# Hymba block with hierarchical mixture of experts: the final norm of all rows moved into the last two experts' products, and those experts' rows gathered, summed, normed and stored over the others

## The chip, the cores and the metric

The kernel runs on one core of a Trainium2 chip. The metric is the device time of one execution in microseconds (us). Engines: PE (TensorE, matmuls; PEld are its weight loads), DVE (VectorE), ACT (ScalarE), POOL (GpSimd), SP (SyncE, which here only issues DMAs). A queue issues its DMAs in the order written; POOL issues the indirect ones (gathers and scatters by a list of row numbers).

## The reference, cut to what matters

One layer over 1024 rows of 1024 numbers: a mixer, a cross attention, then a mixture of experts, and a last RMS norm. Each row goes to one of 4 groups and to 2 of the 4 experts in it, so two experts of different groups never share a row.

```
def hierarchical_moe(h, ...):
    ...
    for e in range(N_EXPERTS):                       # 16
        hid = jax.nn.silu(t @ w_gate[e]) * (t @ w_up[e])
        out = out + combine[:, e:e + 1] * (hid @ w_down[e])
...
    x = x + hierarchical_moe(rms_norm(x, ffn_norm[l]), ...)
return rms_norm(x, final_norm)                       # y * rsqrt(mean(y * y) + eps) * gain
```

## The kernel before, in words

Up to about 780 us the kernel does the mixer, the attention and the routing. It leaves the normed rows in a DRAM buffer `h3d` and the rows so far in a DRAM buffer `acd`, both with 128 spare rows behind the 1024. The experts follow in the order of `ORDER` (L39): 0, 4, 8, 12, 1, ... 3, 7, 11, 15, so neighbours are of different groups. `p` is expert 11 and `LAST` is 15.

An expert takes up to 128 rows as its first slot and up to 64 more as its second; all work of the second slot stands in a branch, `second(e)` (L1207), that is taken only where the expert has more than 128 rows. Empty places of a slot hold row numbers from 1024 up: a gather reads spare rows there, a scatter writes nothing (`bounds_check`). A loop for experts with still more rows (`others`, L1221) isn't entered.

Per expert (loop at L1323): `gate_up` (L1126) for 8 pieces of the gate and up weights, `hidden` (silu and product, L1130), the same for the second slot (`gate_up2`, L1171, `hidden2`), the turning of the next expert's rows, then `down` (L1143) of the expert before, whose 128 weighted rows `add_rows` (L1198) adds into `acd` by an indirect DMA that accumulates; `over` (L1135) turns and splits the hidden rows for `down`; `down2` and `rows2` (L1191, L1194) do the second slot, followed by a second `add_rows`. Each float32 factor is split into a high part (ACT, L163) and a low part (DVE, L169), and a product is three matmuls (`six`, L1119).

The weights are a list of jobs, each a piece of 512 KB. `Weights` (L1260) holds 9 raw buffers (`RAW`) and the other free slots as pairs for split pieces. `load` (L1285) issues on SP while there is a job and a raw buffer; `split(n)` (L1292) splits up to n loaded pieces while a pair is free, gives the raw buffer back and calls `load`. The list (L659) is written out by hand: per expert its 8 gate and up pieces and the 4 down pieces of the expert before; for the last expert the down pieces come first.

`tc.manual_schedule()` (L1312, L1477) keeps each engine's instructions in the order written. The waits between them, DMAs to DRAM included, are put in for every pair of accesses that overlap.

After the loop: down products of 11, its two `add_rows`, then gate and up of 15, the load of all of `acd` into eight tiles `acc` (L1401 to L1403), `over` and down of 15. The rows of 15 aren't added in DRAM: matrices `oh` with a one where row number and slot agree (L1411) place them by matmuls (`placed`, L1433). `MODES` (L57) gives each of the eight tiles a way to the norm: in A DVE adds the placed rows to `acc` (`added`, L1447), ACT squares and sums (L1459), POOL takes the root (L1461), DVE scales and applies the gain `fn` (L1467); in B the add is a matmul with the identity (L1445) and DVE scales from PSUM (L1470). SP stores the tile to `out` (L1475).

Of the kernel before, what the change touches and what calls it, by code (L numbers as in the profile page):

```python
# [8 lines left out]
F32 = mybir.dt.float32  # L9
F32R = mybir.dt.float32r  # L10
# [43 lines left out]
C_N = C_WR + ND * 24  # L54


MODES = "ABABABAB"  # L57
START = 12
FILL = 2
LAG = 2  # L60


class Slots:
# [22 lines left out]
def block_kernel(ctx: ExitStack, tc: tile.TileContext, A):  # L86
# [572 lines left out]
    for s, e in enumerate(ORDER):  # L659
        gu = [("gu", e, k) for k in range(ND)]  # L660
        dn = [("dn", ORDER[s - 1], k) for k in range(4)] if s else []
        for name, i, k in dn + gu if s == NE - 1 else gu + dn:
            W.add((name, i, k), A["w_" + name][i, k])
    for k in range(4):
        W.add(("dn", ORDER[-1], k), A["w_dn"][ORDER[-1], k])
# [541 lines left out]
    def second(e):  # L1207

        return tc.If((flags & (1 << e)) > 0, preferred_fallthrough_block=True)

    hrow = [half.get() for _ in range(2)]
    routed = half.get(BF16, (P, P))
    act.copy(routed, idf)
# [98 lines left out]
    with tc.manual_schedule():  # L1312
        flags = nc.values_load(two[0:1, 0:1], engines=(PE, ACT, DVE), min_val=0, max_val=(1 << NE) - 1)
        X = Weights(W.jobs, W.flying, W.ready, RAW)
        X.load()
        x0 = x0_bufs[0]
        run(turned(x0, xg[0]))
        with second(ORDER[0]):
            turned2()
        for i in range(2):  # L1320
            fetch(ORDER[1], i)
        pool.memset(og[1][LO], 0.0)
        for s, e in enumerate(ORDER[:-1]):  # L1323
            p = ORDER[s - 1] if s else None
            nx = ORDER[s + 1]
            for k in range(ND):
                gate_up(x0, X.get(("gu", e, k)), k)
                X.split(1)
            hidden()
            ws = [X.get(("gu", e, k)) for k in range(ND)]  # L1330
            with second(e):
                for k in range(ND):
                    gate_up2(ws[k], k)
                hidden2(slot(e, 1)[1])
            for k in range(ND):
                X.drop(("gu", e, k))
            x0 = x0_bufs[(s + 1) % 2]
            ops = turned(x0, xg[0])
            if s + 2 < NE:
                fetch(ORDER[s + 2], 0)  # L1340
            run(ops)
            X.split(2)
            if p is not None:
                wd = [X.get(("dn", p, k)) for k in range(4)]
                for k in range(4):
                    down(wd[k], k)
                X.split(1)
                weighted(slot(p, 0)[1])
                add_rows(slot(p, 0)[0], og[0])
            over()  # L1350
            X.split(2)
            if p is not None:
                with second(p):
                    for k in range(4):
                        down2(wd[k], k)
                    rows2(og[1])
                add_rows(slot(p, 1)[0][LO], og[1][LO])
                for k in range(4):
                    X.drop(("dn", p, k))
            with second(e):  # L1360
                over2()
            with second(nx):  # L1362
                turned2()
            if s + 2 < NE:
                fetch(ORDER[s + 2], 1)


        p, LAST = ORDER[-2:]
        wd = [X.get(("dn", p, k)) for k in range(4)]
        for k in range(4):  # L1370
            down(wd[k], k)
        X.split(1)
        weighted(slot(p, 0)[1])
        add_rows(slot(p, 0)[0], og[0])
        with second(p):
            for k in range(4):
                down2(wd[k], k)
            rows2(og[1])
        add_rows(slot(p, 1)[0][LO], og[1][LO])
        for k in range(4):  # L1380
            X.drop(("dn", p, k))
        slots.put(*xg, *x0_bufs[NE % 2])
        fn, row = slots.get(), slots.get()
        oh = slots.get(F32R), slots.get(F32R)
        pool.iota(row, pattern=[[1, T]], base=0, channel_multiplier=0, allow_small_or_imprecise_dtypes=True)
        pool.dma_start(fn, A["final_norm"])
        for k in range(ND):
            gate_up(x0, X.get(("gu", LAST, k)), k)
            X.split(2)
        hidden()  # L1390
        ws = [X.get(("gu", LAST, k)) for k in range(ND)]
        with second(LAST):
            for k in range(ND):
                gate_up2(ws[k], k)
            hidden2(slot(LAST, 1)[1])
        for k in range(ND):
            X.drop(("gu", LAST, k))
        assert not X.jobs
        X.split(4)
        wd = [X.get(("dn", LAST, k)) for k in range(4)]  # L1400
        acc = [X.place(X.raw, F32) for _ in range(NT)]  # L1401
        for t in range(NT):
            sp.dma_start(acc[t], acd[cut(t), :])  # L1403
        over()
        with second(LAST):
            over2()
        slots.put(*x0, xp)
        slots.free.extend(X.raw)
        ogs = [[slots.get(F32R) for _ in range(2)] for _ in range(2)]
        for i in range(2):  # L1410
            dve.tensor_scalar(oh[i], row, idf[:, LAST * 8 + i:LAST * 8 + i + 1], None, op0=ALU.is_equal)  # L1411
        with second(LAST):
            for k in range(4):
                down2(wd[k], k)
            rows2(og[1])
            split(ogs[1][0][LO], ogs[1][1][LO], og[1][LO])
        for k in range(4):
            down(wd[k], k)
        for n in range(2):
            split(ogs[0][0][:, HS[n]], ogs[0][1][:, HS[n]], dn_banks[n], slot(LAST, 0)[1])  # L1420
        for k in range(4):
            X.drop(("dn", LAST, k))
        slots.free.extend(X.pair)
        slots.put(*og, hid, hp)
        banks.put(*gu_banks, *dn_banks, *turn_banks)

    ssf = const.tile([P, 2 * NT], F32, name="ssf")
    rf = const.tile([P, NT], F32, name="rf")  # L1430
    pss, jk = {}, {}

    def placed(t):  # L1433
        jk[t] = slots.get()
        pss[t] = [banks.get() for _ in range(2)]
        for n, ps in enumerate(pss[t]):
            pe.matmul(ps, oh[0][:, cut(t)], ogs[0][0][:, HS[n]], start=True, stop=False)
        with second(LAST):
            for n, ps in enumerate(pss[t]):
                for o in ogs[1]:  # L1440
                    pe.matmul(ps, oh[1][LO, cut(t)], o[LO, HS[n]], start=False, stop=False)
        for n, ps in enumerate(pss[t]):
            pe.matmul(ps, oh[0][:, cut(t)], ogs[0][1][:, HS[n]], start=False, stop=MODES[t] != "B")  # L1443
            if MODES[t] == "B":
                pe.matmul(ps, ident, acc[t][:, HS[n]], start=False, stop=True)  # L1445

    def added(t):  # L1447
        if MODES[t] != "B":
            for n, ps in enumerate(pss[t]):
                dve.tensor_tensor(acc[t][:, HS[n]], ps, acc[t][:, HS[n]], op=ALU.add)  # L1450

    def summed(t):
        r, s2 = rf[:, t:t + 1], [ssf[:, 2 * t + n:2 * t + n + 1] for n in range(2)]
        if MODES[t] == "B":
            for n, ps in enumerate(pss[t]):
                act.activation(jk[t][:, HS[n]], ps, AF.Square, scale=1.0 / 32.0, accum_out=s2[n])  # L1456
            pool.tensor_scalar(r, s2[0], s2[1], EPS, op0=ALU.add, op1=ALU.add)  # L1457
        else:
            act.activation(jk[t], acc[t], AF.Square, scale=1.0 / 32.0, accum_out=s2[0])  # L1459
            pool.tensor_scalar(r, s2[0], EPS, None, op0=ALU.add)  # L1460
        pool.tensor_tensor(r, r, mhalf[:, 0:1], op=ALU.pow)  # L1461
        slots.put(jk[t])

    def scaled(t):
        r = rf[:, t:t + 1]
        if MODES[t] == "A":
            dve.scalar_tensor_tensor(acc[t], acc[t], r, fn, op0=ALU.mult, op1=ALU.mult)  # L1467
        elif MODES[t] == "B":
            for n, ps in enumerate(pss[t]):
                dve.scalar_tensor_tensor(acc[t][:, HS[n]], ps, r, fn[:, HS[n]], op0=ALU.mult, op1=ALU.mult)  # L1470
        else:
            act.activation(acc[t], acc[t], AF.Copy, scale=r)
            pool.tensor_tensor(acc[t], acc[t], fn, op=ALU.mult)
        banks.put(*pss[t])
        sp.dma_start(A["out"][cut(t), :], acc[t])  # L1475

    with tc.manual_schedule():  # L1477
        for t in range(NT + LAG):
            if t < NT:
                placed(t)  # L1480
                added(t)
                summed(t)
            if t >= LAG:
                scaled(t - LAG)


def layout(inputs):
# [63 lines left out]
```

## Time and profile before

| | |
|---|---|
| median of 3 runs | 1225.35 us (1223.7 to 1225.55) |
| the profiled execution | 1224.64 us, of which the span is 1222.9 us |
| PE busy in the span | 1178.0 us, 96% |
| DVE busy | 712.3 us, 58% |
| ACT busy | 567.5 us, 46% |
| POOL busy | 188.6 us, 15% |
| read from HBM, written | 173.49 MB, 29.62 MB |

Times in rows are us from the start of the span. A busy share is an average over stages with different limits; the rows of a stage tell what bounds it. DMA-issuing instructions aren't counted as busy. A wait is put down to the releaser that came last by the profile; where the engine named had long been done, it was another, often a DMA.

### The profile page before, as it was taken

How to read it: one execution, taken by the hardware profiler on the slowest of the kernel's cores; microseconds unless marked ns; L12 is line 12 of the kernel's file. 1: busy time of each engine (PE TensorE's matmuls, PEld its weight loads, DVE VectorE, ACT ScalarE, POOL GpSimd, SP SyncE). 2: the span in 40 equal slices, each digit the busy share in tenths (PEclk: the TensorE clock that was granted, in tenths of full speed). 3: DMA queues.
4: the chain of work that ended last, by engine and by line, in shares of the span. 5: the costliest groups of instructions: out<-in, count | busy, mean ns of one | idle time of the engine just before them, and what ended most of it. 6: DMA issues, size and time to landing. Idle time of an engine off the chain costs nothing. (4 is left out here: it accounts for less than half of the span.)

```text
span 1222.9 us, 20592 instructions
## 1 busy us (share of the span) xinstructions
PE 1178.0 (96%) x7918; PEld 966.8 (79%) x7918; DVE 712.3 (58%) x1162; ACT 567.5 (46%) x965; POOL 188.6 (15%) x229
## 2 busy tenths in 40 slices
PE   9999999999999999999999999789999999999985
PEld 7787878787889988898888888568787777787762
DVE  6625454547457512364454776756867768668645
ACT  6613232323335402463244443545866767658633
POOL 1100101010100100100001333212223222123122
PEclk9999999999999999999999999889999999999988
DMA  9601110111426811120032321667979779798764
GB/s 343 240 18 48 41 54 35 36 53 54 157 85 242 281 63 35 35 104 1 1 121 83 125 104 70 218 232 242 317 245 377 254 263 349 255 338 290 247 176 194
DMA packets 58316, 196.48 MB, mean 161 GB/s; under 512 B 8925, under 2 KB 9565, under 8 KB 58208
## 3 DMA queue, kind: packets, MB, share of 16 engines
q1 hardware_dynamic: 45216, 157.69, 35.2%
q0 software_dynamic: 12704, 37.26, 10.4%
q8 instruction: 68, 1.11, 0.4%
q14 instruction: 40, 0.33, 0.1%
q10 hardware_dynamic: 288, 0.09, 0.0%
HBM read 173.49 MB, written 29.62 MB: 166 GB/s over the span
## 5 line engine op out<-in xcount | busy, mean ns | idle before, releaser
L257 PE MATMUL b<-s,s 128*128 128x512 f32 (+1 forms) x1056 | 402.7, 382 | 0.9 <-ACT s L165 0.8
L259 PE MATMUL b<-s,s 128*128 128x512 f32 (+1 forms) x1056 | 392.6, 372 | 0.0
L258 PE MATMUL b<-s,s 128*128 128x512 f32 (+1 forms) x1056 | 392.1, 371 | 0.1
L169 DVE TENSOR_TENSOR s<-s,s 128x1024 fp32r<-128x1024 f32 (+2 forms) x272 | 315.1, 1203 | 57.1 <-ACT s L163 35.4
L163 ACT CAST s<-s 128x1024 fp32r<-128x1024 f32 (+2 forms) x272 | 268.2, 1042 | 133.5 <-PE b L259 47.7
L1124 PE MATMUL b<-s,s 128*128 128x512 f32 x1152 | 275.3, 397 | 4.5 <-PEq L1362 1.7
L1124 PEld LDWEIGHTS b<-s,s 128*128 128x128 f32 x1152 | 217.0, 191 | 51.9 <-ACT s L163 2.7
L259 PEld LDWEIGHTS b<-s,s 128*128 128x128 f32 x1056 | 199.0, 188 | 35.4 <-issue 0.2
L257 PEld LDWEIGHTS b<-s,s 128*128 128x128 f32 x1056 | 199.0, 189 | 33.5 <-ACT s L165 1.5
L258 PEld LDWEIGHTS b<-s,s 128*128 128x128 f32 x1056 | 199.5, 189 | 31.3 <-DVE s L171 1.0
L169 DVE TENSOR_TENSOR s<-b,s 128x512 fp32r<-128x512 f32 (+1 forms) x112 | 70.9, 647 | 45.5 <-ACT s L163 42.5
L1200 POOL DMA_INDIRECT acd<-s,idi x30 | 59.2, 1972 | 204.9 <-ACT s L1148 66.4
L1163 PE MATMUL b<-s,s 128*128 128x512 f32 x384 | 90.5, 391 | 0.0
L1163 PEld LDWEIGHTS b<-s,s 128*128 128x128 f32 x384 | 71.6, 188 | 14.7
L163 ACT CAST s<-b 128x512 fp32r<-128x512 f32 (+1 forms) x112 | 60.7, 558 | 42.6 <-PE b L264 16.6
L1106 POOL DMA_INDIRECT s<-h3d,idi x32 | 37.1, 1160 | 106.4 <-PE b L1114 87.3
L1175 ACT COPY h<-b 64x512 f32<-64x512 f32 x32 | 18.6, 582 | 67.7 <-PE b L1163 57.0
L1176 DVE TENSOR_TENSOR h<-b,h 64x512 f32<-64x512 f32 x16 | 10.9, 682 | 63.1 <-ACT h L1175 63.1
L784 DVE TENSOR_TENSOR s<-b,s 128x512 f32<-128x512 f32 x16 | 11.0, 691 | 58.7 <-PE b L259 58.6
L264 PE MATMUL b<-ident,s 128*128 128x128 f32 x288 | 40.9, 273 | 1.0 <-DVE s L615 0.9
L547 DVE TENSOR_TENSOR s<-s,s 128x512 f32<-128x512 f32 x28 | 19.3, 691 | 37.6 <-PE b L538 22.1
L264 PEld LDWEIGHTS b<-ident,s 128*128 128x128 f32 x288 | 34.5, 140 | 8.0 <-DVE s L615 1.3
(232 smaller groups left out, 920.2 us busy)
## 6 DMA issues: line engine op xcount, KB each, us to landing
s<-in_w_gu_dram SPq DMA_DIRECT2D x128, 512.0 KB, 6.8
s<-in_w_dn_dram SPq DMA_DIRECT2D x64, 512.0 KB, 7.5
s<-in_w_in_dram SPq DMA_DIRECT2D x26, 512.0 KB, 3.5
s<-in_w_kv_dram SPq DMA_DIRECT2D x16, 512.0 KB, 5.5
h3d<-s POOLq DMA_DIRECT2D x9, 512.0 KB, 3.1
acd<-s POOLq DMA_DIRECT2D x9, 512.0 KB, 3.2
s<-in_xT_dram SPq DMA_DIRECT2D x16, 256.0 KB, 5.5
s<-in_x_dram SPq DMA_DIRECT2D x8, 512.0 KB, 9.0
```

What stands on the lines that cost most here:

```text
L163: act.copy(hi, src)
L169: (eng or dve).tensor_tensor(lo, src, hi.bitcast(F32), op=ALU.subtract)
L257: pe.matmul(ps, lh, rh, start=first, stop=False)
L258: pe.matmul(ps, lh, rl, start=False, stop=False)
L259: pe.matmul(ps, ll, rh, start=False, stop=last)
L264: pe.transpose(pt[:, cut(c)], src[:, cut(half * 4 + c)], ident)
L547: dve.tensor_tensor(k4[:, :, 0, :], k4[:, :, 0, :], tv[:, :, 1:2].to_broadcast([P, nb, w]), op=ALU.mult)
L1106: pool.indirect_dma_start(out=to, out_offset=None, in_=h3d, in_offset=rows, bounds_check=T - 1, oob_is_err=False)
L1124: pe.matmul(ps[n], l, r[:, HS[n]], start=a, stop=b)
L1163: pe.matmul(ps[n], l, r[:, HS[n]], start=first and i == 0, stop=last and i == 1)
L1175: act.copy(up2[UP], ps[UP])
L1200: pool.indirect_dma_start(out=acd, in_=src, in_offset=None, compute_op=ALU.add, out_offset=rows, bounds_check=T - 1, oob_is_err=False)
```

## The change

The final norm's modes are now A (as before, but with nothing to add) and C: ACT scales by the root, POOL multiplies by the gain. The weights of 11's down product move behind 15's gate and up pieces. The down product of 11 moves behind gate and up of 15. Four tiles of `acc` take the slots of the gathered rows and of the turned rows that are no longer needed, four more take raw weight buffers as these come free; `residual` loads them from `acd`, which by then lacks the rows of 11 and 15. Those experts' rows are gathered out of `acd` into `ax` (four gathers), the weighted products are added there (`first_sum`, `second_sum`), and they are normed by themselves (`again` names their columns, `first_out`, `second_out`); `store` writes them with indirect DMAs over the rows that the eight tiles' stores have written. The one-hot matrices, `placed` and `added` go, and with them 11's `add_rows`. The functions of the tail that are removed are those printed above (`placed` to the end, L1429 to L1484); they stand as "..." in the diff.

```
@@ -54,10 +54,9 @@
 C_N = C_WR + ND * 24
 
 
-MODES = "ABABABAB"
+MODES = "ACACACAC"
 START = 12
 FILL = 2
-LAG = 2
 
 
 class Slots:
@@ -659,7 +658,7 @@
     for s, e in enumerate(ORDER):
         gu = [("gu", e, k) for k in range(ND)]
         dn = [("dn", ORDER[s - 1], k) for k in range(4)] if s else []
-        for name, i, k in dn + gu if s == NE - 1 else gu + dn:
+        for name, i, k in gu + dn:
             W.add((name, i, k), A["w_" + name][i, k])
     for k in range(4):
         W.add(("dn", ORDER[-1], k), A["w_dn"][ORDER[-1], k])
@@ -1208,6 +1207,9 @@
 
         return tc.If((flags & (1 << e)) > 0, preferred_fallthrough_block=True)
 
+    ssf = const.tile([P, NT + 8], F32, name="ssf")
+    rf = const.tile([P, NT + 4], F32, name="rf")
+    pool.memset(ssf, 1.0)
     hrow = [half.get() for _ in range(2)]
     routed = half.get(BF16, (P, P))
     act.copy(routed, idf)
@@ -1365,28 +1367,96 @@
                 fetch(ORDER[s + 2], 1)
 
 
+
         p, LAST = ORDER[-2:]
-        wd = [X.get(("dn", p, k)) for k in range(4)]
-        for k in range(4):
-            down(wd[k], k)
-        X.split(1)
-        weighted(slot(p, 0)[1])
-        add_rows(slot(p, 0)[0], og[0])
-        with second(p):
-            for k in range(4):
-                down2(wd[k], k)
-            rows2(og[1])
-        add_rows(slot(p, 1)[0][LO], og[1][LO])
-        for k in range(4):
-            X.drop(("dn", p, k))
+        assert p // 4 != LAST // 4
         slots.put(*xg, *x0_bufs[NE % 2])
-        fn, row = slots.get(), slots.get()
-        oh = slots.get(F32R), slots.get(F32R)
-        pool.iota(row, pattern=[[1, T]], base=0, channel_multiplier=0, allow_small_or_imprecise_dtypes=True)
-        pool.dma_start(fn, A["final_norm"])
+        acc = [slots.get() for _ in range(4)]
+
+        def residual(ts):
+            for t in ts:
+                sp.dma_start(acc[t], acd[cut(t), :])
+
+        def root(r, *ss):
+            if len(ss) == 2:
+                pool.tensor_scalar(r, ss[0], ss[1], EPS, op0=ALU.add, op1=ALU.add)
+            else:
+                pool.tensor_scalar(r, ss[0], EPS, None, op0=ALU.add)
+            pool.tensor_tensor(r, r, mhalf[0:r.shape[0], 0:1], op=ALU.pow)
+
+        def squares(a, ss):
+            act.activation(jk[0:a.shape[0], 0:a.shape[1]], a, AF.Square, scale=1.0 / 32.0, accum_out=ss)
+
+        def summed(t):
+            squares(acc[t], ssf[:, t:t + 1])
+            root(rf[:, t:t + 1], ssf[:, t:t + 1])
+
+        def scaled(t):
+            r = rf[:, t:t + 1]
+            if MODES[t] == "A":
+                dve.scalar_tensor_tensor(acc[t], acc[t], r, fn, op0=ALU.mult, op1=ALU.mult)
+            else:
+                act.activation(acc[t], acc[t], AF.Copy, scale=r)
+                pool.tensor_tensor(acc[t], acc[t], fn, op=ALU.mult)
+            sp.dma_start(A["out"][cut(t), :], acc[t])
+
+        def final(ts):
+            for i, t in enumerate(ts):
+                summed(t)
+                if i:
+                    scaled(ts[i - 1])
+            scaled(ts[-1])
+
+        def again(j, i):
+
+            c = NT + 2 * j + i
+            return rf[:, c:c + 1], [ssf[:, NT + 4 * j + 2 * i + n:NT + 4 * j + 2 * i + n + 1] for n in range(2)]
+
+        def first_sum(j, e):
+            a, (r, ss) = ax[j][0], again(j, 0)
+            for n in range(2):
+                dve.scalar_tensor_tensor(a[:, HS[n]], dn_banks[n], slot(e, 0)[1], a[:, HS[n]],
+                                         op0=ALU.mult, op1=ALU.add)
+                squares(a[:, HS[n]], ss[n])
+            root(r, *ss)
+
+        def second_sum(j, e, wd):
+            a, (r, ss) = ax[j][1][LO], again(j, 1)
+            with second(e):
+                for k in range(4):
+                    down2(wd[k], k)
+                rows2(og[1])
+                dve.tensor_tensor(a, a, og[1][LO], op=ALU.add)
+                squares(a, ss[0][LO])
+            root(r[LO], ss[0][LO])
+
+        def store(ix, src):
+            rows = bass.IndirectOffsetOnAxis(ap=ix, axis=0)
+            pool.indirect_dma_start(out=A["out"], in_=src, in_offset=None, out_offset=rows,
+                                    bounds_check=T - 1, oob_is_err=False)
+
+        def first_out(j, e):
+            a, r = ax[j][0], again(j, 0)[0]
+            dve.scalar_tensor_tensor(a, a, r, fn, op0=ALU.mult, op1=ALU.mult)
+            store(slot(e, 0)[0], a)
+
+        def second_out(j, e):
+            a, r = ax[j][1][LO], again(j, 1)[0]
+            with second(e):
+                dve.scalar_tensor_tensor(a, a, r[LO], fn[LO], op0=ALU.mult, op1=ALU.mult)
+            store(slot(e, 1)[0][LO], a)
+
         for k in range(ND):
             gate_up(x0, X.get(("gu", LAST, k)), k)
-            X.split(2)
+            X.split(1)
+            if not X.jobs and len(acc) == 4:
+                residual(range(4))
+            if len(X.raw) >= 5 and len(acc) == 4:
+                acc += [X.place(X.raw, F32) for _ in range(4)]
+                residual(range(4, NT))
+                fn = X.place(X.raw, F32)
+                pool.dma_start(fn, A["final_norm"])
+        assert not X.jobs and len(acc) == NT
         hidden()
         ws = [X.get(("gu", LAST, k)) for k in range(ND)]
         with second(LAST):
@@ -1395,93 +1465,33 @@
             hidden2(slot(LAST, 1)[1])
         for k in range(ND):
             X.drop(("gu", LAST, k))
-        assert not X.jobs
         X.split(4)
-        wd = [X.get(("dn", LAST, k)) for k in range(4)]
-        acc = [X.place(X.raw, F32) for _ in range(NT)]
-        for t in range(NT):
-            sp.dma_start(acc[t], acd[cut(t), :])
+        wd, wl = ([X.get(("dn", e, k)) for k in range(4)] for e in (p, LAST))
+        slots.free.extend((*X.pair, *X.raw))
+        jk = slots.get()
+        ax = [[slots.get() for _ in range(2)] for _ in range(2)]
+        for j, e in enumerate((p, LAST)):
+            for i in range(2):
+                ix, to = (slot(e, 1)[0][LO], ax[j][1][LO]) if i else (slot(e, 0)[0], ax[j][0])
+                pool.indirect_dma_start(out=to, out_offset=None, in_=acd,
+                                        in_offset=bass.IndirectOffsetOnAxis(ap=ix, axis=0))
+        final(range(0, 3))
+        for k in range(4):
+            down(wd[k], k)
         over()
+        first_sum(0, p)
+        second_sum(0, p, wd)
         with second(LAST):
             over2()
-        slots.put(*x0, xp)
-        slots.free.extend(X.raw)
-        ogs = [[slots.get(F32R) for _ in range(2)] for _ in range(2)]
-        for i in range(2):
-            dve.tensor_scalar(oh[i], row, idf[:, LAST * 8 + i:LAST * 8 + i + 1], None, op0=ALU.is_equal)
-        with second(LAST):
-            for k in range(4):
-                down2(wd[k], k)
-            rows2(og[1])
-            split(ogs[1][0][LO], ogs[1][1][LO], og[1][LO])
+        final(range(3, NT))
+        first_out(0, p)
+        second_out(0, p)
+        second_sum(1, LAST, wl)
+        second_out(1, LAST)
         for k in range(4):
-            down(wd[k], k)
-        for n in range(2):
-            split(ogs[0][0][:, HS[n]], ogs[0][1][:, HS[n]], dn_banks[n], slot(LAST, 0)[1])
-        for k in range(4):
-            X.drop(("dn", LAST, k))
-        slots.free.extend(X.pair)
-        slots.put(*og, hid, hp)
-        banks.put(*gu_banks, *dn_banks, *turn_banks)
...
+            down(wl[k], k)
+        first_sum(1, LAST)
+        first_out(1, LAST)
```

## Rows read from the trace of the kernel before

**Rows 1.** The page's first line: the span.
```profile
span 1222.9 us, 20592 instructions
```
**Rows 2.** Windows: stretch, length, busy PE, PEld, DVE, ACT, POOL, clock, DMA, GB/s.
```profile
1150.00:1180.00 30.00, 27.34 (x120) 21.16 (x118) 19.09 (x22) 20.53 (x27) 7.14 (x5) 1.00 0.48 123
...
1193.00:1213.00 20.00, 16.72 (x48) 8.41 (x48) 15.28 (x20) 10.18 (x25) 6.88 (x15) 1.00 0.53 214
```
**Rows 3.** Timeline of PE: start, us, line, operation, count, idle before.
```profile
1157.14 5.95 PE L1124 MATMUL b<-s,s 128*128 128x512 f32 x24 [0.42 <-ACT s L163]
...
1162.93 3.79 PE L1163 MATMUL b<-s,s 128*128 128x512 f32 x16
...
1166.56 5.60 PE L1124 MATMUL b<-s,s 128*128 128x512 f32 x24
...
1184.71 7.73 PE L1124 MATMUL b<-s,s 128*128 128x512 f32 x24 [0.72 <-ACTq L1405]
```
**Rows 4.** The stores to out: issue in ns, first and last start; landing.
```profile
L1475 SPq DMA_DIRECT2D out_dram<-s x8: 332/332/451, 1201.6 to 1215.1; - x8
...
DMA to landing us min/median/max: 2.6/2.7/3.3
```
**Rows 5.** Timeline of SP's DMA issues, from 1156.
```profile
1156.49 4.33 SPq L1289 DMA_DIRECT2D s<-in_w_dn_dram  x4
...
1183.53 5.05 SPq L1403 DMA_DIRECT2D s<-acd  x8
```
**Rows 6.** Waits of SP's queue: us in total, times, longest.
```profile
SPq L1403 <- DMA acd<-s,idi: 22.3, 1, 22.3
```
**Rows 7.** Timeline of POOL: expert 7's second row addition, expert 11's first.
```profile
1167.85 1.43 POOL L1200 DMA_INDIRECT acd<-s,idi  x1 [8.81 <-DMA acd<-s,idi]
...
1171.11 1.56 POOL L1200 DMA_INDIRECT acd<-s,idi  x1 [1.82 <-DMA acd<-s,idi]
```
**Rows 8.** Windows of 2 us while the eight loads of acc run.
```profile
1186.00:1188.00 2.00, 2.00 (x6) 1.52 (x6) 0.95 (x2) 0.00 (x0) 0.00 (x0) 0.50 1.10 309
...
1190.00:1192.00 2.00, 2.00 (x10) 1.66 (x9) 0.00 (x0) 0.00 (x0) 0.00 (x0) 1.00 1.02 416
```
**Rows 9.** DMA queues from 1100 to 1150: packets, MB, share of 16 engines.
```profile
q1 hardware_dynamic: 3456, 12.58, 65.4%
...
q0 software_dynamic: 896, 2.32, 19.4%
```
**Rows 10.** Groups by line and shape: busy us, mean ns of one, idle before.
```profile
L169 DVE TENSOR_TENSOR s<-s,s 128x1024 fp32r<-128x1024 f32 x14 | 16.2, 1215 | 0.7 <-ACT s L163 0.4 <-DVEq L1362 0.3
...
L1459 ACT ACTIVATE s<-s 128x1024 f32<-128x1024 f32 x4 | 4.2, 1057 | 7.7 <-DVE s L1450 6.0 <-issue 1.8
...
L1459 ACT ACTIVATION_READ_ACCUMULATOR s<-s 128x1 f32 x4 | 0.7, 186 | 0.0
...
L1461 POOL TENSOR_TENSOR rf<-rf,mhalf 128x1 f32<-128x1 f32 x8 | 4.5, 565 | 0.7
...
L1467 DVE SCALAR_TENSOR_TENSOR s<-s,rf,s 128x1024 f32<-128x1024 f32 x4 | 5.1, 1276 | 0.0
...
L171 DVE SCALAR_TENSOR_TENSOR s<-b,wts,s 128x512 fp32r<-128x512 f32 x2 | 1.4, 746 | 6.0 <-ACT s L165 6.0
...
L961 POOL TENSOR_TENSOR s<-s,s 128x512 f32<-128x512 f32 x8 | 10.4, 1302 | 8.3 <-ACT s L960 8.3
...
L1175 ACT COPY h<-b 64x512 f32<-64x512 f32 x3 | 1.7, 582 | 2.3 <-DVE s L1176 2.3
```
**Rows 11.** Issue to landing, us: gathers, additions at 1167.85 and 1171.11, acc loads.
```profile
s<-h3d,idi POOLq DMA_INDIRECT x2, 4.6
...
acd<-s,idi POOLq DMA_INDIRECT x1, 2.5
...
acd<-s,idi POOLq DMA_INDIRECT x1, 6.2
...
DMA to landing us min/median/max: 5.6/8.2/10.1
```

More of the change, by code (lines that the diff above doesn't have):

```diff
@@ L1417, in block_kernel @@
-        for k in range(4):
-            down(wd[k], k)
-        for n in range(2):
-            split(ogs[0][0][:, HS[n]], ogs[0][1][:, HS[n]], dn_banks[n], slot(LAST, 0)[1])
-        for k in range(4):
-            X.drop(("dn", LAST, k))
-        slots.free.extend(X.pair)
-        slots.put(*og, hid, hp)
-        banks.put(*gu_banks, *dn_banks, *turn_banks)
[L1429 to L1484, printed above, removed]
+        final(range(3, NT))
[3 more added lines that the diff above has]
+        second_out(1, LAST)
+        for k in range(4):
+            down(wl[k], k)
+        first_sum(1, LAST)
+        first_out(1, LAST)
 def layout(inputs):
```

## The prediction, made before the change was run

> **What bounds the kernel now.** I read the page first: 1222.9 us of span [rows 1]. The profiled execution took 1224.64 us, so 1.74 us lie around the span, and it stands 0.71 us below the 1225.35 us median. All sums below are made against 1224.64. About 0.2%, 2.4 us, is what a measurement can tell from no change.
>
> Next I read the windows by stage. Until 1180 PE is busy 27.3 of 30 us; from 1193 to 1213 it shares the work with DVE at 15.3 of 20 [rows 2]. The change touches only what follows 1157, so the PE rows from there come third: the products of expert 11 (the kernel's `p`, 24 big matmuls and 16 for its second rows), the first half of expert 15's gate and up, and, after a break, expert 15's down product at half clock, 7.73 us [rows 3]. Expert 15 (`LAST`) has no second rows: no L1163 follows. After 1193 comes the tail that the change replaces: placing by one-hot products, norm, stores; the last store is issued at 1215.1 and the span ends 7.8 us later [rows 4].
>
> Then the queues. SP issues its last weight load by 1160.8 and nothing more until 1183.5 [rows 5]; it is held 22.3 us there, by the landing of the last row addition into `acd` [rows 6]. POOL shows why: each addition starts only when the one before it has landed [rows 7].
>
> **What goes.** The eight placings (48 matmuls), `added`, and the two one-hot builds: from 1193 to 1215, 22 us on the path. Expert 11's two row additions, from 1171.1 on, go too, so the rows of `acd` are final when expert 7's second addition lands, at 1171.1 [rows 7]. The products close up: gate and up of 15 from 1157.1 take 11.2 us (two halves of 5.6), down of 11 takes 5.9, its second rows 3.8 [rows 3], so PE is free near 1178. If nothing else held it, down of 15 would end near 1184, 8 us earlier than now. The new order of the weight list costs nothing: as many loads and splits come at each place, and seven of 15's eight pieces are already split when the loop ends. Without that cover each piece would cost a split, 1.2 us on DVE. The memset of 16 columns lies beside the routing; the iota and the one-hot builds that go were on no path.
>
> **What comes first: the loads of `acc`.** Follow `residual(range(4))` through the gate and up loop of 15. Its condition is that no weight is left to issue and that `acc` still has four tiles. The weight list is empty before the loop begins [rows 5]. Raw buffers were all in flight; each turn frees one, so five are free only in the fifth turn, when `acc` grows. The condition is therefore true in turns one to five, and the same four loads are issued **five times**: 20 loads of 0.524 MB, then the other four, where eight were issued before. Each repeat overwrites the same tile, so it waits for the load before it to land, and the first norm waits for the fifth. Nothing else is queued behind SP but the stores.
>
> Time of acc[0]: start at 1171.2, when the addition has landed. Sixteen loads and its own make 17. The rate where SP's loads are alone on the DMA engines is 416 GB/s [rows 8], so 1.26 us each, 21.4 us; four in flight cover the reissue. Fixed part: a store of the same size lands in 2.7 us [rows 4], so 1.4 besides its transfer. POOL's four gathers move 384 rows, 1.57 MB, on the same engines; in an earlier stretch POOL's queue took 19.4% for 2.32 MB where SP's took 65.4% for 12.58 [rows 9], over 50 us that is 4.2 against 2.6 us a MB, so 6.6 us (4.1 at SP's price). `final_norm` lands before. acc[0] is ready at 1171.2 + 21.4 + 1.4 + 6.6 = 1200.6; the lower bound is 1197, from the gathers at SP's price and one of them before the loads. Here a rule speaks for a later time. The Trainium skill, DMA: Bandwidth & Descriptors, section Where 436 GB/s comes from, says that transfers between HBM and SBUF are bound at about 358 GB/s. By it acc[0] would be ready 3.6 us later; the row disagrees, and the row is used.
>
> **What waits for acc[0].** The engines run in written order. ACT's first norm square stands ahead of `over`, both sums and the later norms, so ACT, then DVE and POOL, hold still from about 1172 to 1200.6. PE does down of 11 and its second rows, then waits for ACT's split of 15's hidden rows, some 25 us; its clock was at half after the break before down of 15 too [rows 8], where the 24 matmuls took 7.73 us for 5.95 [rows 3]. A longer break may make it 10 us; it lies beside work that ends later.
>
> **The tail from acc[0], T0.** Durations [rows 10]: square 1.06 + 0.19; root 0.57, with the small add before it and handoffs 0.9; scaling on DVE 1.28; ACT's copy is taken as the square's 1.06. POOL's multiply by `fn` has no row at 1024 columns; twice the 512-column row is 2.6 (0.4 either way, an estimate: a start shared by the halves, or DVE beside it). Three squares and a copy: 5.0. `over` and the halves of `first_sum` of 11 (0.75 on DVE, 0.78 on ACT): 9.3. The branch, two second-row sums (0.58 on ACT, at most 0.75 on DVE), an add of 1.2, a square of 1.25, the untaken branch: T0 + 15.6. Then five tiles, held by POOL: two squares 2.5, copy 1.2, multiply 2.7, root 0.9, copy 1.2, multiply 2.6, root 0.9, copy 1.2, multiply 2.6, in all 15.8, and store and landing 2.8: T0 + 34.2. The Trainium skill, GPSIMD Engine Reference, section Elementwise — side-by-side cycle accounting, states 4497 ns for 2048 columns; half of it, 2.25 us as an estimate, would end the tail 1.0 us sooner. No row here shows that size.
>
> Then four scatters into `out`. They overlap all stores to `out`, as the additions overlap in `acd`, so the first waits for the last store and each for the one before. A plain scatter has no row. Nearest: a plain gather lands 4.6 us after issue, an addition that writes no row 2.5 (3.3 between starts), an adding scatter of 128 rows 6.2 [rows 7, 11]. I take 4.6 with 0.3 of handoff, 4.4 for 64 rows; bounds 3.3 and 6.2. Eleven's two: 9.3. Fifteen's second scatter writes no row, 1.4 of POOL; the last root is queued behind it, 1.2, then DVE's scaling 1.3 and the last scatter 4.6. The last row lands at T0 + 51.9. From the last landing to the span's end it was 5.1 us (7.8 less 2.7) [rows 4].
>
> **Sum:** 1200.6 + 51.9 + 5.1 = 1257.6 of span, + 1.74 = **1259 us**, 2.8% slower. The work removed from the path (22 us) is outweighed: the norms start 22 us after the products of 11, and the tail behind their start is 57 us.
>
> **Rivals.** (a) Each round waits out a whole landing. The eight loads of before landed in a median 8.2 us, the first in 5.6 [rows 11]; four rounds of 8.2 and one of 5.6 give acc[0] at 1209.6: 1268. For it: reissue needs a semaphore and SP's turn. Against: four in flight hold 5 us of transfer, more than 2.7.
> (b) Scatters into `out` are not held by the stores or by each other, since no row shows an order on `out`: the last lands at T0 + 44.2, 1252. Against: [rows 7].
> (c) The other side: the loads are issued once, that is, five raw buffers are free in the first turn. Its place is the first pass of the condition, its price 25.5 us: acc[0] at 1175, and 1234 with my tail. The length of the tail decides: up to 45 us after acc[0] (mine is 51.9) it ends within 0.2% of before, and with the short scatters of (b), 44.2, at **1226, not slower**. For it: eight loads would do all the work. Against: the count of free buffers, and SP's rows [rows 5].
> (d) Multiply and scatters at their upper bounds: T0 + 56.8, 1264.
>
> **Numbers.** Forecast with its bounds 0.60; (a) 0.12; (b) 0.12; (c) 0.07, of which 0.03 within 0.2% and 0.02 faster; (d) 0.07; 0.02 faster for what I have not seen. So faster 0.04, same 0.03, slower 0.93. The forecast's bounds are -3.5 for the loads and -5.2 to +4.9 for the tail; (a) reaches 1268; (b), with the gathers wholly ahead of the loads (-6.6) and the multiply low (-1.2), 1244. The range is 1243 to 1269.
>
> **What would show it.** SP issues 24 loads from `acd`, with about 25 us of waits on their own landings; ACT, DVE and POOL stand still from about 1172 to 1200; PE has one gap of over 20 us before down of 15, at half clock after it; POOL's three multiplies lead the five norms; four scatters close the chain, POOL waiting for DMA. Eight loads, or a first square before 1180, would make the step on the loads wrong; scatters that start before the last store lands, the step on their order.

## The result, and the profile after

Median 1266.71 us (1266.33 to 1267.62, 4 runs) against 1224.53 us (1221.64 to 1225.55, 4 runs) for the kernel before on the same chip: ratio 1.035, 95% interval 1.033 to 1.0369. The forecast was 1259 us, with a range of 1243 to 1269. The profiled execution is the one of 1267.62 us; 1.8 us of it lie around the span. Its page begins:

```profile
span 1265.8 us, 20509 instructions
```

against [rows 1]. The windows by stage, in the columns of [rows 2]:

```profile
1180.00:1190.00 10.00, 0.28 (x2) 0.00 (x0) 0.00 (x0) 0.00 (x0) 0.00 (x0) 0.67 1.02 317
1190.00:1200.00 10.00, 0.00 (x0) 0.00 (x0) 0.00 (x0) 0.00 (x0) 0.00 (x0) 0.50 1.01 392
1200.00:1206.00 6.00, 0.00 (x0) 0.00 (x0) 0.00 (x0) 0.00 (x0) 0.00 (x0) 0.50 1.02 410
1206.00:1243.00 37.00, 7.38 (x24) 5.47 (x24) 15.52 (x14) 19.13 (x33) 22.70 (x24) 0.59 0.50 200
1243.00:1266.00 23.00, 0.00 (x0) 0.00 (x0) 1.28 (x1) 0.00 (x0) 5.71 (x8) 0.50 0.15 53
```

For 26 us no engine computes and the DMA engines are full: the kernel waits for data. Then follow 37 us in which no engine is full, POOL the busiest, and 23 us of almost nothing. The timeline of SP, where [rows 5] had eight loads in 5.05 us:

```profile
1174.72 32.57 SPq L1378 DMA_DIRECT2D s<-acd  x24
1209.78 30.01 SPq L1401 DMA_DIRECT2D out_dram<-s  x8
```

and the waits of SP's queue, in the columns of [rows 6]:

```profile
SPq L1378 <- DMA s<-acd: 23.2, 16, 3.2
...
SPq L1378 <- DMA acd<-s,idi: 11.3, 1, 11.3
```

There are 24 loads, and 16 of them wait for the load of the same tile before them: four tiles, five times each. The wait on the row addition has halved against [rows 6], and a longer one on loads stands behind it. Timeline of ACT: the first norm square, whose bracket is the idle time before it.

```profile
1206.29 1.06 ACT L1388 ACTIVATE s<-s 128x1024 f32<-128x1024 f32 x1 [33.39 <-DMA s<-acd]
```

Timeline of PE: the last three products, where [rows 3] had 11's down product ahead of gate and up of 15.

```profile
1170.46 5.71 PE L1123 MATMUL b<-s,s 128*128 128x512 f32 x24
...
1176.37 3.92 PE L1162 MATMUL b<-s,s 128*128 128x512 f32 x16
1214.17 7.38 PE L1123 MATMUL b<-s,s 128*128 128x512 f32 x24 [33.89 <-DVE s L1418]
```

PE stands still for 33.9 us. Down of 15 follows; its granted clock is 0.50 from 1214 to 1216, the lower of PE's two levels, and 1.00, the higher, from 1218 to 1222. It takes 7.38 us, near the 7.73 of [rows 3]; it ends at 1221.55, beside the norms, and DVE takes up its product only at 1236.02, so it costs nothing. Timeline of POOL: its multiplies and the four scatters (L1435).

```profile
1211.75 3.23 POOL L1400 TENSOR_TENSOR s<-s,s 128x1024 f32<-128x1024 f32 x1 [0.30 <-ACT s L1399]
...
1224.34 3.36 POOL L1400 TENSOR_TENSOR s<-s,s 128x1024 f32<-128x1024 f32 x1 [0.16 <-ACT s L1399]
...
1229.91 3.21 POOL L1400 TENSOR_TENSOR s<-s,s 128x1024 f32<-128x1024 f32 x1 [0.30 <-ACT s L1399]
1233.21 1.08 POOL L1384 TENSOR_SCALAR rf<-ssf 128x1 f32<-128x1 f32 x1
1234.38 1.46 POOL L1385 TENSOR_TENSOR rf<-rf,mhalf 128x1 f32<-128x1 f32 x1
1237.09 2.34 POOL L1400 TENSOR_TENSOR s<-s,s 128x1024 f32<-128x1024 f32 x1 [1.26 <-ACTq L1425]
1243.22 1.09 POOL L1435 DMA_INDIRECT out_dram<-s,idi  x1 [3.78 <-issue]
1247.47 0.93 POOL L1435 DMA_INDIRECT out_dram<-s,idi  x1 [3.16 <-issue]
...
1251.41 0.98 POOL L1435 DMA_INDIRECT out_dram<-s,idi  x1 [2.06 <-DMA out_dram<-s,idi]
...
1255.03 1.05 POOL L1435 DMA_INDIRECT out_dram<-s,idi  x1 [1.61 <-DVE s L1440]
```

The scatters start about 4 us apart, the first 3.8 us after the last multiply's end: it waits for the stores, says the view of their line L1401 (who waited for it: us, times), and the view of L1435 has the scatters' own landings.

```profile
  POOL out_dram L1435: 3.8, 1
```
```profile
DMA to landing us min/median/max: 2.0/3.3/3.5
```

The chain of waits ends with them: scatter, wait, scatter. The last one lands 3.4 us after its issue, and the span ends 7.4 us after that.

### The profile page after: what moved, and what is told of

It reads as the page before. It is cut to its first block, busy times and chain, and to the rows that moved or that the text cites. A ratio compares the mean times of both kernels' runs of the same rounds, so it can differ in the third digit from the quotient of the medians.

```text
span 1265.8 us, 20509 instructions
## 1 busy us (share of the span) xinstructions
PE 1162.2 (92%) x7870; PEld 959.3 (76%) x7870; DVE 709.1 (56%) x1150; ACT 572.5 (45%) x967; POOL 205.4 (16%) x247
## 3 DMA queue, kind: packets, MB, share of 16 engines
q0 software_dynamic: 13376, 39.34, 10.2%
## 5 line engine op out<-in xcount | busy, mean ns | idle before, releaser
L1123 PE MATMUL b<-s,s 128*128 128x512 f32 x1152 | 275.8, 398 | 36.4 <-DVE s L1418 33.9
L258 PEld LDWEIGHTS b<-s,s 128*128 128x128 f32 x1056 | 199.0, 188 | 35.3 <-issue 0.2
L1199 POOL DMA_INDIRECT acd<-s,idi x28 | 52.7, 1884 | 199.2 <-ACT s L1147 78.2
```

What stands on the lines that cost most here:

```text
L258: pe.matmul(ps, ll, rh, start=False, stop=last)
L1123: pe.matmul(ps[n], l, r[:, HS[n]], start=a, stop=b)
L1199: pool.indirect_dma_start(out=acd, in_=src, in_offset=None, compute_op=ALU.add, out_offset=rows, bounds_check=T - 1, oob_is_err=False)
```

## The experiments

The theory: the loss is three things behind each other, namely sixteen needless loads, norms slowed by POOL, and serial scatters. The first four kernels each take one of these away, or part of one. The kernel before took 1222.25 us (median of 7 runs) beside these four. A time without a range and a ratio is that of a single run, and so less certain.

**Loads once.**
```
-            if not X.jobs and len(acc) == 4:
+            if not X.jobs and len(acc) == 4 and k == 0:
```


> One edit: the loads of the first four tiles are issued in the first turn alone, eight loads instead of 24. Theory (the repeats move 8.4 MB ahead of the first norm, and every us of that is on the path): the first norm square starts near 1179 in place of 1206.3, some 27 us earlier, and the time falls from 1267 to about 1240, still slower than the kernel before by over 1%, since the tail behind the first norm keeps its length of about 52 us to the last landing. Rival 1 (POOL's gathers, which land 8.8 to 12 us after 1175, hold the first norm as well): first square at 1187 or later, 1248. Rival 2 (the end is held by something else than the loads): no change, 1267.

Measured: 1239.82 us (1239.48 to 1240.33, 4 runs), ratio 1.0141 (1.0124 to 1.0158). Timelines of SP and ACT of this kernel:

```profile
1173.03 5.09 SPq L1378 DMA_DIRECT2D s<-acd  x8
```
```profile
1177.57 1.06 ACT L1388 ACTIVATE s<-s 128x1024 f32<-128x1024 f32 x1 [5.98 <-DMA s<-acd]
```

The first norm comes 4.5 us after the first load instead of 31.6, and 27 of the 42 us are gone. The gathers don't hold the first norm here. The span still ends 60.9 us after that square (59.5 in the changed kernel): the rest of the loss is in the tail.

**Three rounds of loads.**
```
-            if not X.jobs and len(acc) == 4:
+            if not X.jobs and len(acc) == 4 and k >= 2:
```


> The same loads issued three times instead of five, 16 loads in all. Theory (each round costs its transfer, 2.1 MB at 400 GB/s, 5.3 us): 10.5 us less than 1267, about 1256.5. Rival (only the number of rounds that still run beside POOL's gathers counts, or only the last wait): less than 4 us, 1263 or more.

Measured: 1258.22 us, 8.5 less for two rounds, 4.2 a round, below the 5.3 expected; SP's loads start at 1173.72 and the first square comes at 1196.87, 23.2 us later against 31.6. Timelines of SP and ACT, and two windows of this kernel:

```profile
1173.72 24.53 SPq L1378 DMA_DIRECT2D s<-acd  x16
```
```profile
1196.87 1.06 ACT L1388 ACTIVATE s<-s 128x1024 f32<-128x1024 f32 x1 [24.70 <-DMA s<-acd]
```
```profile
1192.00:1194.00 2.00, 0.00 (x0) 0.00 (x0) 0.00 (x0) 0.00 (x0) 0.00 (x0) 0.50 0.89 305
1194.00:1196.00 2.00, 0.00 (x0) 0.00 (x0) 0.00 (x0) 0.00 (x0) 0.00 (x0) 0.50 0.91 311
```

From one round (4.5 us) to three it is 9.3 a round. So rounds don't cost the same: the early ones share the DMA engines with the four gathers (317 GB/s from 1180 to 1190, against 410 from 1200, in the windows above), the later ones run at full rate, where 2.1 MB take 5.1 us. That two rounds fewer save 8.5 us and not 10.2 is explained in part: here the end of the last round ran at 305 to 311 GB/s, which costs about 1 us against 410. Why it did, and the rest, stays open.

**No multiplies on POOL.**
```
-MODES = "ACACACAC"
+MODES = "AAAAAAAA"
```


> Five rounds kept; all eight tiles scaled on DVE, so POOL multiplies nothing and ACT copies nothing. Theory (POOL's multiplies, 3.2 to 3.4 us beside DVE, lead the last five norms): the five norms take about 9 us from their first square to the last store's issue in place of 18.6, and the time falls by 9 to 10 us to about 1257.5. Rival (DVE takes the place of POOL, or the scatters wait for something else): less than 3 us, 1264 or more.

Measured: 1261.17 us, 5.5 less, where 9 were expected. From first square to span end it is 53.9 us instead of 59.5. Timelines of ACT, DVE and POOL of this kernel:

```profile
1205.55 1.06 ACT L1388 ACTIVATE s<-s 128x1024 f32<-128x1024 f32 x1 [33.76 <-DMA s<-acd]
```
```profile
1225.44 1.28 DVE L1397 SCALAR_TENSOR_TENSOR s<-s,rf,s 128x1024 f32<-128x1024 f32 x1 [0.77 <-POOL rf L1385]
1227.49 1.28 DVE L1397 SCALAR_TENSOR_TENSOR s<-s,rf,s 128x1024 f32<-128x1024 f32 x1 [0.77 <-POOL rf L1385]
```
```profile
1222.48 0.22 POOL L1384 TENSOR_SCALAR rf<-ssf 128x1 f32<-128x1 f32 x1 [0.46 <-ACT s L1388]
...
1225.49 1.31 POOL L1384 TENSOR_SCALAR rf<-ssf 128x1 f32<-128x1 f32 x1
...
1227.54 1.31 POOL L1384 TENSOR_SCALAR rf<-ssf 128x1 f32<-128x1 f32 x1
```

A tile takes 2.05 us, not DVE's 1.28. POOL's small add, 0.22 us alone, takes 1.31 when it starts beside a scaling and ends with it (1225.49 + 1.31 = 1226.80; 1225.44 + 1.28 = 1226.72). The next scaling waits for that root, so DVE and POOL take turns.

**One scatter less.** Left out is the store of 15's second slot, which holds no row here.
```
         second_sum(1, LAST, wl)
-        second_out(1, LAST)
         first_sum(1, LAST)
```


> Five rounds and modes kept; the scaling and the scatter of expert 15's second slot are left out (the slot holds no rows in these inputs, so no row of the output is missing). Theory (each scatter waits until the one before it has landed): the last scatter starts one step earlier, about 3.6 us less, 1263.5. Rival (scatters are not held by one another, POOL's own time alone counts): 1.0 us less, 1266.5.

Measured: 1261.39 us, 5.3 less. Timelines of SP and ACT of this kernel:

```profile
1171.15 33.65 SPq L1378 DMA_DIRECT2D s<-acd  x24
```
```profile
1203.17 1.06 ACT L1388 ACTIVATE s<-s 128x1024 f32<-128x1024 f32 x1 [33.64 <-DMA s<-acd]
```

This run began its loads 3.6 us sooner than the changed kernel although the code up to there is the same, so I count from the first square: 56.4 us to the span's end instead of 59.5, 3.1 less. The scatters are serial, and one without a row costs the path 3 us. (That offset also shows how far one run's stages can shift.)

**All three.** Loads once, all A, 15's empty store left out as above.

> The three single edits together: loads issued once, all tiles scaled on DVE, no scatter for the empty second slot of expert 15. Theory (they lie one behind the other on one chain): the gains add, 26.9 for the loads, 5.6 and 3.1 from the first norm on, so 1231 against 1266.7, still slower than the kernel before by 0.7%. Rival (with the loads early, one of the others is hidden): 1235 or more.

Measured: 1231.81 us, beside 1223.25 for the kernel before. The parts add up: 27 + 5.5 + 3 from 1266.7 give 1231.2. What is left, 8.6 us, is the change without these three: the gathers, the norms of 11's and 15's rows apart from the others, and three serial scatters behind all stores. How it divides among them was not measured.

The next kernels ask what the idea is worth without them. Only 15's rows are now done late; 11's row additions into `acd` are back where they were, all eight tiles are loaded once behind them, and two gathers and two scatters remain:
```
+        add_rows(slot(p, 0)[0], og[0])
...
+        add_rows(slot(p, 1)[0][LO], og[1][LO])
...
-        ax = [[slots.get() for _ in range(2)] for _ in range(2)]
-        for j, e in enumerate((p, LAST)):
...
+        ax = [[None, None], [slots.get(), slots.get()]]
+        residual(range(NT))
...
+        final(range(4, NT))
         second_sum(1, LAST, wl)
         second_out(1, LAST)
```
The first takes all tiles by way A:

> Expert 11 is undone: its down products come first again and its rows are added in DRAM, then all eight tiles are loaded once; only expert 15's rows are gathered and scattered, behind the norms; all tiles scaled on DVE. Theory: the loads start at 1183 as in the kernel before, land by 1196; DVE's scaling and POOL's root take turns, 2.05 us a tile, from 1190 to 1206; stores land at 1209, the two scatters (2.2 and 3.5) at 1215, the end 7.4 later: 1222 of span, 1224, within 0.5% of before. Rival (DVE and POOL do not hold each other up, the loads set the pace): 1218.

Measured: 1227.70 us (1226.22 to 1228.46, 5 runs), ratio 1.0034 (1.0019 to 1.0048), 3.7 us above the 1224 of the theory, though within its 0.5%. The norms run at 2.05 us a tile here too, but for one gap, in the timeline of DVE:

```profile
1200.46 1.28 DVE L1412 SCALAR_TENSOR_TENSOR s<-s,rf,s 128x1024 f32<-128x1024 f32 x1 [3.19 <-POOL rf L1400]
```

POOL issues the two gathers between the fourth and the fifth root, and DVE waits 3.2 us for the root behind them, where it waits 0.77 for the others.

In the second every other tile is copied to PSUM by PE, which has nothing left to do once 15's down product is done, and DVE scales it from there:
```
-MODES = "AAAAAAAA"
+MODES = "ABABABAB"
...
+                    pe.matmul(ps[n], ident, acc[t][:, HS[n]], start=True, stop=True)
...
+                    dve.scalar_tensor_tensor(acc[t][:, HS[n]], pst[t][n], r, fn[:, HS[n]], op0=ALU.mult, op1=ALU.mult)
```


> The same, but every second tile goes through PSUM by a matmul with the identity on the idle PE and is scaled from there on DVE. Theory (a DVE instruction that reads one operand from PSUM leaves POOL's root free, so the pair takes 1.28 + 1.49 on DVE in place of 4.1): the norms end some 4 us earlier than with all tiles from SBUF, 1220 against 1224, faster than the kernel before by about 0.2 to 0.5%. Rival (the hold-up is not from the SBUF operands): no difference to the run with all tiles on DVE, or slower by the halves' own cost, 0.2 us a tile.

Measured: 1226.02 us (1224.69 to 1227.84, 10 runs), ratio 1.0028 (1.0019 to 1.0038), a miss of 6 us. The norms did get shorter, as the theory said: from the first scaling to the end of the last it is 13.8 us instead of 18.1. But that end, at 1202.6, doesn't set the time. Timeline of POOL, its two scatters:

```profile
1208.55 1.00 POOL L1459 DMA_INDIRECT out_dram<-s,idi  x1 [6.51 <-issue]
...
1212.21 1.06 POOL L1459 DMA_INDIRECT out_dram<-s,idi  x1 [1.62 <-DVE s L1464]
```

The first goes out only at 1208.55, after 6.5 us of POOL waiting: stores, loads and gathers fill the DMA engines (405 GB/s from 1188 to 1206), and the scatter needs the last store landed. That first scatter is the empty one of the second slot; the one with the rows follows 3.7 us later.

**Empty work not issued.** Gather, root and scatter of 15's second rows go into the branch that only experts with such rows take; POOL reads the flag too.
```
+        flags4 = nc.values_load(two[0:1, 0:1], engines=(PE, ACT, DVE, POOL), min_val=0, max_val=(1 << NE) - 1)
...
-            with second(e):
+            with tc.If((flags4 & (1 << e)) > 0, preferred_fallthrough_block=True):
...
-            store(slot(e, 1)[0][LO], a)
+                store(slot(e, 1)[0][LO], a)
```


> The previous variant with alternating matrix-and-VectorE norms, in which GpSimd too reads the flag that tells whether expert 15 has second rows: the gather, the root and the scatter of those rows, which hold nothing here, stand inside the branch. My theory (scatters into out come one behind the other, and an empty one costs its full 3.7 us, since the root of the first rows is queued behind it): the root of the first rows comes at 1206 instead of 1210, one scatter remains, issued as soon as the last store has landed, near 1209, and the span ends 3.5 us sooner: median near 1222.5, level with the kernel before at 1223. Rival: the end is set by the last store's landing and the wait behind it alone, or GpSimd's branch costs what the scatter did: median stays near 1226.

Measured: 1222.79 us (1221.49 to 1223.83, 11 runs), ratio 0.9994 (0.9985 to 1.0003): as forecast, level with the kernel before.

**Empty additions not issued.** The loads wait for a chain of additions [rows 6, 7], and 7's second writes no row. With that step in a branch of POOL's own, once in the kernel above and once in the kernel before, which has nothing of the change:
```
+        flagsP = nc.values_load(two[0:1, 0:1], engines=(POOL,), min_val=0, max_val=(1 << NE) - 1)
...
-                add_rows(slot(p, 1)[0][LO], og[1][LO])
+                with tc.If((flagsP & (1 << p)) > 0, preferred_fallthrough_block=True):
+                    add_rows(slot(p, 1)[0][LO], og[1][LO])
```


> The variant with the branch for expert 15's second rows, and in addition the row additions of the second rows into acd stand in a branch that GpSimd alone takes, so that an empty one (expert 7's, among others) is not issued. My theory: the loads of acc wait for a chain of serial additions into acd, in which 7's empty second addition holds 11's first for 3.3 us between starts. Without it 11's additions come some 2.5 us sooner, the loads start near 1179.7 instead of 1182.2, the tail behind them keeps its length, and the median falls to about 1220.3, some 0.2 to 0.3% below the kernel before. Rival: the tail is set by ACT's and DVE's splits of 15's weights and hidden rows, not by the loads: no change, 1222.8.

> The kernel before with the same branch of GpSimd around the second row additions, and nothing of the change. In it too the loads of acc wait 22.3 us for the last addition. If the additions' chain sets the tail, it gains the same 2 to 3 us: near 1221. If its placing products on PE set it, since they wait for 15's down product rather than for the loads, it stays at 1223.5. The one tells whether a gain of the other variant belongs to the change's idea or to the branch.

Measured: 1219.05 us (1218.09 to 1220.65, 6 runs), ratio 0.9962 (0.9949 to 0.9974), for the variant of the change, and 1222.65 us (1220.31 to 1224.66, 11 runs), ratio 0.9991 (0.9981 to 1.0001), for the kernel before with the branch. So the variant beats both kernels, and by 3.6 us the one with the branch alone. The timeline of POOL and that of SP in the variant:

```profile
1155.48 2.14 POOL L1199 DMA_INDIRECT acd<-s,idi  x1 [15.54 <-ACT s L1147]
1166.86 1.55 POOL L1199 DMA_INDIRECT acd<-s,idi  x1 [9.24 <-ACT s L1147]
1173.74 1.94 POOL L1199 DMA_INDIRECT acd<-s,idi  x1 [5.33 <-DVE s L168]
...
1206.29 1.06 POOL L1464 DMA_INDIRECT out_dram<-s,idi  x1 [2.79 <-issue]
```
```profile
1179.01 4.54 SPq L1396 DMA_DIRECT2D s<-acd  x8
1186.72 13.16 SPq L1428 DMA_DIRECT2D out_dram<-s  x8
```

Three additions where there were four, and the loads start 23.5 us after the first of them; without this branch it was 26.3 (1155.88 to 1182.21). The last store is issued at 1199.9, 15 us sooner than in [rows 4], and one scatter behind it gives most of that back. In the kernel before with the branch the loads come sooner too, 23.3 us after the first addition (26.6 without it), but its tail doesn't hang on them. Timelines of SP and of ACT of that kernel:

```profile
1182.48 4.65 SPq L1405 DMA_DIRECT2D s<-acd  x8
```
```profile
1192.87 1.27 ACT L165 ACTIVATE s<-b,wts 128x512 fp32r<-128x512 f32 x2 [8.46 <-PE b L1124]
```

Placing starts when PE's down product of 15 is done, whenever `acc` is there. That product does end sooner with the branch, by some 1.7 us in the two traces (33.6 against 35.3 us after the start of 11's): it starts 2.5 us sooner but takes 8.60 us for the 7.73 of [rows 3]. So a gain of up to 0.2% isn't excluded for this kernel; its interval doesn't show one.

## Why the prediction was right, and where its sizes were off

The mechanism held: "the norms start 22 us after the products of 11" (measured: 26, from 1180.3 to 1206.3), "and the tail behind their start is 57 us" (59.5). Term by term, in us, counted in the profiled execution:

| step of the prediction | predicted | measured | off |
|---|---|---|---|
| rows of `acd` final, loads start | 1171.2 | 1174.7 | +3.5 |
| loads until acc[0] (21.4 + 1.4 + 6.6) | 29.4 | 31.6 | +2.2 |
| acc[0] to the last store's landing | 34.2 | 36.9 | +2.7 |
| four scatters to the last landing | 17.7 | 15.2 | -2.5 |
| last landing to the end of the span | 5.1 | 7.4 | +2.3 |

With 0.1 around the span that is +8.3, from 1259.3 to 1267.6.

That the time still lies within the range is luck in part. The prediction says "The forecast's bounds are -3.5 for the loads and -5.2 to +4.9 for the tail", which ends at 1264.2; 1266.7 is 2.5 us beyond. The range reached to 1269 only because rival (a) reaches 1268, and (a) is refuted below. The start, the loads and the end had no bound on the late side, and they are 3.5, 2.2 and 2.3 us late; the scatters, priced too high, gave 2.5 back.

**The start.** About 2 us of the +3.5 are the run: the product that PE starts at 1157.14 in [rows 3] has its place at 1159.15 here. In the other kernels with the same code up to there that place is at 1155.8 to 1158.4, so a shift of this size is ordinary. The rest is 7's second addition, which landed 4.2 us after its issue, for 2.5 in [rows 11].

**The five rounds.** The step "true in turns one to five" was right: 24 issues, 16 waits. The count came from the code, no row of before could show it. The rate was right as well: 5.1 us a round against 4 x 1.26. The Trainium skill's 358 GB/s, which the prediction set against its row (DMA: Bandwidth & Descriptors, section Where 436 GB/s comes from), doesn't fit here either: 392 and 410 GB/s stand in the windows. That section works the figure out as half of what a memory stack gives to two cores; here one core runs. The term that was too small is the one for the four gathers: 31.6 less 21.4 and 1.4 leaves 8.8 us for its 6.6. This is a remainder and no price of the gathers: worked out in the same way it is 10.4 us with three rounds and 1.9 with one.

**The rivals.** (a) gives 1268, nearer to the time than the forecast, and is still wrong: a round that waits out a landing of 8.2 us would have saved 16.4 with two rounds gone, and 8.5 were saved; nor is any of the 16 waits longer than 3.2 us. (b) falls by the scatters' starts, 4 us apart, and by the 3.1 us that one of them was worth. (c), loads once, would be 1234 with the predicted tail; made in earnest it is 1239.8. A first square 2.6 us later than its 1175 and a tail 3.9 longer than the predicted 57 make the difference; both are counted in the profiled run, which took 1240.3. Its "not slower" needed at most 45 us from acc[0] to the last landing, and it is 53.6 (from 1177.57 to the last scatter at 1227.74 and 3.4 of landing). (d) named the multiply and the scatters together: the one was slow, the other fast.

**The tail.** "POOL's multiply, 2.6" was mis-sized, and not as a size of its own: alone it takes 2.34, beside DVE 3.2 to 3.4. Beside it stand DVE's scalings with two SBUF inputs (last section), and one root lost 1.75 us in the same way (1.08 + 1.46 for 0.22 + 0.57). The multiply alone is near the 2.25 us that the prediction worked out from the Trainium skill, GPSIMD Engine Reference, section Elementwise — side-by-side cycle accounting. The scatters were over-priced by gathers as the nearest row: they land in 2.0 to 3.5 us, the gathers of [rows 11] in 4.6. PE's gap, taken as some 25 us up to ACT's split of 15's hidden rows, was 33.9, and its end is put down to DVE's sums of 11's rows (L1418) behind that split; neither is on the path.

**The end.** After a last DMA of POOL's queue the span went on for 7.4 us (6.9 in the fastest variant), after a last store of SP's for 5.1 [rows 4]. Why was not tried.

So most of the loss comes from how the change places its work: 27 us are loads repeated by a condition, 5.5 the multiplies on POOL, 3 an empty scatter. Without these three the change as a whole is still 0.7% slower (the single run of all three). This rest goes, and some 5 us more, only in a kernel that gives up half of the idea: 11's rows stay in the early additions, half of the tiles pass through PSUM, and the empty work of 15 and 7 isn't issued.

## What to carry to other kernels

A condition that triggers an issue inside a loop must also record that it has issued: count the DMAs of the changed kernel by hand before believing what it does. Rows that are written over other rows by an indirect DMA wait here for all the stores under them and for each other, about 4 us each and some 3 even when empty, so leave as few as possible for the end and put empty ones into a branch that their issuing engine takes. Two changes that show no gain alone can pay together: the shorter chain of additions gave nothing clear of noise to the kernel before (0.9981 to 1.0001), where the products set the tail, and some 3.7 us to the kernel whose tail starts with the loads.

## What the runs showed of the hardware that was not expected

POOL and DVE hold each other up by operand, not by being busy. Timelines of DVE and POOL in the last variant, where tiles of both ways alternate:

```profile
1191.90 1.28 DVE L1421 SCALAR_TENSOR_TENSOR s<-s,rf,s 128x1024 f32<-128x1024 f32 x1
1193.09 1.40 DVE L1424 SCALAR_TENSOR_TENSOR s<-b,rf,s 128x512 f32<-128x512 f32 x2
```
```profile
1192.17 1.09 POOL L1402 TENSOR_SCALAR rf<-ssf 128x1 f32<-128x1 f32 x1
...
1193.99 0.22 POOL L1402 TENSOR_SCALAR rf<-ssf 128x1 f32<-128x1 f32 x1
```

Beside the scaling whose two tensors lie in SBUF (`s<-s,rf,s`) the small add takes 1.09 us and ends when the scaling does; beside the one that reads PSUM (`s<-b,rf,s`) it takes 0.22 and ends while DVE is still busy. The two scalings differ in width too, 1024 and 512 columns; no run separates that. The Trainium skill, GPSIMD Engine Reference, section Key points, says that GpSimd shares its SBUF interfaces with VectorE and contends with VectorE instructions that have two SBUF inputs; the trace agrees. It goes the other way as well. Timeline of DVE in the changed kernel, a scaling of the same size as those of 1.28:

```profile
1230.85 3.36 DVE L1440 SCALAR_TENSOR_TENSOR s<-s,rf,s 128x1024 f32<-128x1024 f32 x1
```

It began inside POOL's multiply of 1229.91 to 1233.12, and ended at 1234.21, 1.1 us behind the multiply, which is nearly the whole of its own 1.28.
